# Average pooling over windows of four: an output tile with 64 KB stores on one queue, against three in-place input tiles with 16 KB stores on a second queue

## The chip, the core and the metric

The kernel runs on one core of a Trainium2 chip. The metric is the device time of one execution in microseconds. The core has 16 DMA engines that move data between the chip's memory (HBM) and the 128 partitions of its on-chip memory (SBUF); VectorE and ScalarE compute on what lies in SBUF. A DMA is issued by an instruction in the queue of some engine: SyncE (SP), which does nothing else here, or ScalarE. Instructions of one engine's queue are issued in order, and one that waits for a semaphore holds up all that stand behind it on the same engine.

## The reference

```python
x = np.random.randn(64, 256, 8192).astype(np.float32)   # kernel_size 4, stride 4
out_len = (length - kernel_size) // stride + 1
for i in range(out_len):
    start = i * stride
    output[:, :, i] = np.mean(x[:, :, start : start + kernel_size], axis=2)
```

Each output is the mean of four neighbouring floats, and the windows do not overlap. Since 8192 is a multiple of 4, rows need no special treatment: the input is one long list of floats, and output number j is the mean of inputs 4j to 4j + 3. 536.87 MB are read and 134.22 MB are written.

## The kernel before, in words

The 16384 rows of x are dealt to 128 partitions so that each partition holds 1,048,576 floats in all. The work is cut into 16 groups, and each group into 4 blocks (`LOADS`) of W = 16384 floats, 64 KB, per partition. In a group a partition owns 8 consecutive rows of x, 256 KB, and the views `xg` and `og` (lines 43 to 47) put them behind one another. So a load of one block (line 59) reads 64 KB from each of 128 places that lie 256 KB apart.

There are two input tiles (`xin`, line 49) and a single output tile (`res`, line 50), 64 KB per partition each. `sums` (lines 62 to 83) works on one block: VectorE adds neighbours, writing the 8192 results over the first half of the input tile (line 65), then adds neighbours of these into the block's quarter of the output tile (line 72). ScalarE scales the quarter by 1/4 in place (line 83). In the last block of a group the second sum and the scaling are cut in four, so that less remains after the last sum. Then one store (line 86) writes the whole output tile, 64 KB per partition, 8 MB.

All DMAs, loads and stores, are issued by SP (lines 59 and 86). The order there is written out by the loop of lines 97 to 112: the sums of block k, after a group's last block the store of the group, and then the load of block k + 2, which must wait until the sums of block k are done, as it takes their tile. The next group's second sum waits until the store has left the output tile. The DMA engines take what SP issued in the order of issue.

The end is cut finer. The last block is loaded in five pieces (line 92). The output of the last group's first two blocks is stored between the first and second of these loads (line 109); the third block's output is stored after the loads have been issued (line 114), which gives the DMA engines work while the last pieces are summed. The last two pieces are scaled on VectorE (line 79) and stored by the last instruction (line 121).

The lines that matter below are 59 (loads), 65 and 72 (the sums), 83 (the scaling) and 86 (the stores). Line 152 is the end of the program and line 138 its beginning.

Of the kernel before, what the change touches and what calls it, by code (L numbers as in the profile page):

```python
# [1 line left out]

# [4 lines left out]


LOADS = 4

LAST_CUTS = 4


@with_exitstack
def kernel(
    ctx: ExitStack,
    tc: tile.TileContext,
    x: bass.AP,
    kernel_size: bass.AP,
    stride: bass.AP,  # L20
    out: bass.AP,
):
    nc = tc.nc
    K, S = int(kernel_size), int(stride)
    assert K == S == 4
    B, C, L = x.shape
    P = nc.NUM_PARTITIONS
    add = mybir.AluOpType.add
    dt = x.dtype

    per = B * C * L // P
    W = 16384
    G = W * LOADS
    V = W // K
    groups = per // G
    assert per == groups * G

    xf = x.flatten_outer_dims()
    of = out.flatten_outer_dims()
    rows = G // L  # L40
    R = P * rows

    def xg(g):
        return xf[g * R : (g + 1) * R].rearrange("(p f) m -> p (f m)", f=rows)

    def og(g):
        return of[g * R : (g + 1) * R].rearrange("(p f) m -> p (f m)", f=rows)

    pin = ctx.enter_context(tc.tile_pool(name="xin", bufs=2))
    pout = ctx.enter_context(tc.tile_pool(name="res", bufs=1))  # L50

    state = {}

    def load(g, l, a, b):

        if a == 0:
            state["xt"] = pin.tile([P, W], dt, name="xt")
        xt = state["xt"]
        nc.sync.dma_start(out=xt[:, a:b], in_=xg(g)[:, l * W + a : l * W + b])  # L59
        return xt  # L60

    def sums(xt, ot, l, a, b, cuts, scale_on_dve=False):

        h = (a, (a + b) // 2)
        nc.vector.tensor_tensor(  # L65
            out=xt[:, h[0] : h[1]], in0=xt[:, a:b:2], in1=xt[:, a + 1 : b : 2], op=add
        )
        n = (b - a) // K
        for c in range(cuts):
            lo, hi = c * n // cuts, (c + 1) * n // cuts  # L70
            o = ot[:, l * V + a // K + lo : l * V + a // K + hi]
            nc.vector.tensor_tensor(  # L72
                out=o,
                in0=xt[:, a + 2 * lo : a + 2 * hi : 2],
                in1=xt[:, a + 2 * lo + 1 : a + 2 * hi : 2],
                op=add,
            )
            if scale_on_dve:
                nc.vector.tensor_scalar(  # L79
                    out=o, in0=o, scalar1=1.0 / K, scalar2=None, op0=mybir.AluOpType.mult  # L80
                )
            else:
                nc.scalar.mul(o, o, 1.0 / K)  # L83

    def store(g, ot, a, b):
        nc.sync.dma_start(out=og(g)[:, a:b], in_=ot[:, a:b])  # L86

    todo = [(g, l) for g in range(groups) for l in range(LOADS)]  # L90
    last = todo[-1]
    pieces = [W // 2, W // 4, W // 8, W // 16, W // 16]
    tiles = {}
    ot = None
    tiles[0] = load(*todo[0], 0, W)
    tiles[1] = load(*todo[1], 0, W)
    for k, (g, l) in enumerate(todo[:-1]):
        if l == 0:
            held, ot = ot, pout.tile([P, G // K], dt, name="ot")
        sums(tiles.pop(k), ot, l, 0, W, LAST_CUTS if l == LOADS - 1 else 1)  # L100
        if l == LOADS - 1:
            store(g, ot, 0, G // K)
        if k + 2 < len(todo) - 1:
            tiles[k + 2] = load(*todo[k + 2], 0, W)
        elif k + 2 == len(todo) - 1:

            n = pieces[0]
            lt = load(*last, 0, n)
            store(g, ot, 0, (l + 1) * V)
            for w in pieces[1:]:  # L110
                load(*last, n, n + w)
                n += w
    g, l = last
    store(g, ot, (l - 1) * V, l * V)
    edges = [sum(pieces[:i]) for i in range(len(pieces) + 1)]
    for a, b in zip(edges[:3], edges[1:4]):
        sums(lt, ot, l, a, b, 1)
    store(g, ot, l * V, l * V + edges[3] // K)
    for a, b in zip(edges[3:-1], edges[4:]):
        sums(lt, ot, l, a, b, 1, scale_on_dve=True)  # L120
    store(g, ot, l * V + edges[3] // K, (l + 1) * V)


# [1 line left out]
_INS = ['x', 'kernel_size', 'stride']  # L125
_OUTS = [((64, 256, 2048), 'float32')]

_NUMBERS = {'kernel_size': 4, 'stride': 4}


# [26 lines left out]
```

## Time and profile before

| what | value |
|---|---|
| three runs | 1558.01, 1558.77, 1560.35 us (median 1558.77) |
| the profiled execution's own time | 1560.02 us |
| its span, first to last instruction | 1558.2 us |
| ScalarE, line 83, 128x4096 | 48 times, 3616 ns each |
| VectorE, line 65, 128x8192 | 63 times, 8693 ns each |
| VectorE, line 72, 128x4096 | 48 times, 4425 ns each |
| median time from issue to landing, full loads | 26.9 us |
| the same, the 15 large stores | 24.5 us |

The profile is of one execution. Times inside it count from the start of the span; the run's own time is 1.8 us longer than the span. The DMA lines of the page give, for 40 equal slices of the span, the busy share of the 16 DMA engines in tenths. A "packet" there is one contiguous piece that one DMA engine moves: with these layouts one partition's part of a transfer is one packet, so a load of 8 MB is 128 packets of 64 KB, eight on each engine. At the end of its part of a transfer an engine writes a packet of four bytes that counts up a semaphore; those are the 1392 packets under 512 bytes, 16 for each of 87 transfers. The trace has a record of start, duration, queue and size for each packet.

### The profile page before, as it was taken

To read this page: it belongs to the slowest core of one execution; us is meant where nothing else is said; L and a number is where in the kernel's file an instruction comes from. 1 tells how busy PE (TensorE), PEld (TensorE's weight loads), DVE (VectorE), ACT (ScalarE), POOL (GpSimd) and SP (SyncE) were. 2 spreads that over 40 slices of the span, in tenths; PEclk is the share of its full clock that TensorE was granted. 3 is DMA by queue.
4 is the path that set the end of the run, shared out by engine and by line. 5 is a ranking of instruction groups with operands and counts; after the bars stand their busy time and mean duration, and the time that the engine had idled before them with its cause. 6 is when DMAs were issued, how large, how long until landed. Compare 5 with 4: busy or idle time off the path is not lost.

```text
span 1558.2 us, 522 instructions
## 1 busy us (share of the span) xinstructions
DVE 844.0 (54%) x183; ACT 241.9 (16%) x112; POOL 0.2 (0%) x4
## 2 busy tenths in 40 slices
DVE  3654636546365463654636546365463654636546
ACT  1111201112011120111201112011120111201111
POOL 0000000000000000000000000000000000000000
DMA  9999999999999999999999999999999999999998
GB/s 424 437 404 431 442 434 436 434 431 434 429 432 432 439 436 434 432 434 431 431 431 436 436 439 431 434 432 434 431 431 431 431 431 431 431 432 436 426 440 369
DMA packets 12532, 671.13 MB, mean 431 GB/s; under 512 B 1392, under 2 KB 1392, under 8 KB 1776
## 3 DMA queue, kind: packets, MB, share of 16 engines
q1 hardware_dynamic: 12528, 671.09, 99.8%
q14 instruction: 4, 0.03, 0.0%
HBM read 536.87 MB, written 134.22 MB: 431 GB/s over the span
## 4 chain that ended last, share of the span: by engine, by line
DMA 71%; DVE 27%; ACT 1%; SPq 0%; issue 0%
DMA xt<-in_x_dram 71%; DVE xt L65 18%; DVE ot L72 9%; ACT ot L83 1%; SPq L86 0%; SPq L59 0%; DVE ot L79 0%
## 5 line engine op out<-in xcount | busy, mean ns | idle before, releaser
L65 DVE TENSOR_TENSOR xt<-xt 128x8192 f32<-128x8192 f32 (+2 forms) x68 | 556.9, 8190 | 542.5 <-DMA xt<-in_x_dram 542.5
L83 ACT ACTIVATE ot<-ot 128x1024 f32<-128x1024 f32 (+3 forms) x111 | 240.6, 2167 | 1306.1 <-DVE ot L72 1302.6
L72 DVE TENSOR_TENSOR ot<-xt 128x1024 f32<-128x1024 f32 (+4 forms) x113 | 286.9, 2572 | 164.1 <-DMA out_dram<-ot 162.4
L83 ACT ACT_TABLE_LOAD x1 | 1.3, 1283 | 0.7 <-PEq L138 0.7
L79 DVE TENSOR_SCALAR ot<-ot 128x256 f32<-128x256 f32 x2 | 0.6, 291 | 0.0
L138 POOL MEMSET const-bfloat16-1.0<- 128x1 bf16 x1 | 0.1, 101 | 0.0
L138 POOL MEMSET const-uint8-127<- 128x1 uint8 x1 | 0.1, 101 | 0.0
L138 POOL MEMSET const-float32-0.0<- 128x1 f32 x1 | 0.1, 98 | 0.2 <-issue 0.2
L138 POOL MEMSET const-float32-1.0<- 128x1 f32 x1 | 0.1, 98 | 0.0
## 6 DMA issues: line engine op xcount, KB each, us to landing
xt<-in_x_dram SPq DMA_DIRECT2D x1, 4096.0 KB, 17.0
out_dram<-ot SPq DMA_DIRECT2D x1, 4096.0 KB, 23.0
xt<-in_x_dram SPq DMA_DIRECT2D x1, 2048.0 KB, 27.4
out_dram<-ot SPq DMA_DIRECT2D x1, 2048.0 KB, 18.4
out_dram<-ot SPq DMA_DIRECT2D x1, 1792.0 KB, 8.0
xt<-in_x_dram SPq DMA_DIRECT2D x1, 1024.0 KB, 29.4
xt<-in_x_dram SPq DMA_DIRECT2D x2, 512.0 KB, 30.6
xt<-in_x_dram SPq DMA_DIRECT2D x63, 26.9
```

Source lines behind the costliest of these rows:

```text
L65: nc.vector.tensor_tensor(out=xt[:, h[0] : h[1]], in0=xt[:, a:b:2], in1=xt[:, a + 1 : b : 2], op=add)
L72: nc.vector.tensor_tensor(out=o, in0=xt[:, a + 2 * lo : a + 2 * hi : 2], in1=xt[:, a + 2 * lo + 1 : a + 2 * hi : 2], op=add,)
L79: nc.vector.tensor_scalar(out=o, in0=o, scalar1=1.0 / K, scalar2=None, op0=mybir.AluOpType.mult)
L83: nc.scalar.mul(o, o, 1.0 / K)
L138: nc = _bacc.Bacc("TRN2", target_bir_lowering=False, num_devices=1)
```

## The change

The output tile goes, and with it groups. There are three input tiles of 64 KB (`BUFS_IN`), and both sums and the scaling of a block work inside its own tile: the block's 4096 means end up in the tile's first quarter. From there each block is stored by itself, 16 KB per partition, 2 MB in all. The store is issued from ScalarE's queue, right behind the scaling. SP issues the loads, and only two of the last stores: those of the last full block and of the first piece of the last block, which stand behind all loads.

A load now takes the tile of the block three earlier, so it waits for that block's store to have left. The loads run up to two blocks ahead of the block that is summed; once the first piece of the last block is loaded, the other pieces are issued at once.

The input is seen as one flat list. A block is 128 x 16384 consecutive floats, 64 KB for each partition, and the partitions' parts follow one another without gaps; the same holds for the stores, with 16 KB. The last block is cut in pieces of 8192, 4096, 2048, 1280 and 768 floats (before: 8192, 4096, 2048, 1024, 1024), each a contiguous block of its own, all in one tile. Only the last piece is scaled on VectorE.

The core of the diff (the old functions, printed above, go):

```diff
-LOADS = 4
-LAST_CUTS = 4
...
-    pin = ctx.enter_context(tc.tile_pool(name="xin", bufs=2))
-    pout = ctx.enter_context(tc.tile_pool(name="res", bufs=1))
...
+FULL = 16384
+BUFS_IN = 3
+HEAD = ()
+TAIL = (8192, 4096, 2048, 1280, 768)
+    assert L % K == 0
+    dt = x.dtype
+    xf = x.rearrange("b c l -> (b c l)")
+    of = out.rearrange("b c l -> (b c l)")
+    rest = B * C * L // P - sum(HEAD) - sum(TAIL)
+    assert rest % FULL == 0
+    blocks = [(w, i == 0) for i, w in enumerate(HEAD)]
+    blocks += [(FULL, True)] * (rest // FULL)
+    blocks += [(w, i == 0) for i, w in enumerate(TAIL)]
+    n = len(blocks)
+    first = n - len(TAIL)
+    pin = ctx.enter_context(tc.tile_pool(name="xin", bufs=BUFS_IN))
+    xs, begins = {}, [0]
+    for w, _ in blocks:
+        begins.append(begins[-1] + w)
+    def load(i):
+        w, fresh = blocks[i]
+        if fresh:
+            load.tile, load.at = pin.tile([P, FULL], dt, name="xt"), 0
+        a = load.at
+        load.at += w
+        src = xf[P * begins[i] : P * begins[i + 1]].rearrange("(p m) -> p m", p=P)
+        xs[i] = load.tile[:, a : a + w]
+        nc.sync.dma_start(out=xs[i], in_=src)
+    def means(i):
+        w, _ = blocks[i]
+        xt = xs.pop(i)
+        o = xt[:, : w // K]
+        nc.vector.tensor_tensor(out=xt[:, : w // 2], in0=xt[:, ::2], in1=xt[:, 1::2], op=add)
+        nc.vector.tensor_tensor(
+            out=o, in0=xt[:, : w // 2 : 2], in1=xt[:, 1 : w // 2 : 2], op=add
+        )
+        if i == n - 1:
+            nc.vector.tensor_scalar(
+                out=o, in0=o, scalar1=1.0 / K, scalar2=None, op0=mybir.AluOpType.mult
+            )
+        else:
+            nc.scalar.mul(o, o, 1.0 / K)
+        return o
+    def store(engine, i, o):
+        dst = of[P * begins[i] // K : P * begins[i + 1] // K]
+        engine.dma_start(out=dst.rearrange("(p m) -> p m", p=P), in_=o)
+    loaded = 0
+    for i in range(n):
+        while loaded < n and (loaded < i + BUFS_IN or loaded > first):
+            load(loaded)
+            loaded += 1
+        o = means(i)
+        store(nc.sync if i in (first - 1, first) else nc.scalar, i, o)
```

More of the change, by code (lines that the diff above doesn't have):

```diff
@@ L26 @@
     B, C, L = x.shape
+    assert L % K == 0
     P = nc.NUM_PARTITIONS
+    dt = x.dtype
     add = mybir.AluOpType.add
[L29 to L47, printed above, removed]
@@ L49 @@
-    pin = ctx.enter_context(tc.tile_pool(name="xin", bufs=2))
-    pout = ctx.enter_context(tc.tile_pool(name="res", bufs=1))
[L52 to L64, printed above, removed]
+    xf = x.rearrange("b c l -> (b c l)")
@@ L65, in sums @@
+    def means(i):
[3 more added lines that the diff above has]
+        nc.vector.tensor_tensor(out=xt[:, : w // 2], in0=xt[:, ::2], in1=xt[:, 1::2], op=add)
         nc.vector.tensor_tensor(
-            out=xt[:, h[0] : h[1]], in0=xt[:, a:b:2], in1=xt[:, a + 1 : b : 2], op=add
+            out=o, in0=xt[:, : w // 2 : 2], in1=xt[:, 1 : w // 2 : 2], op=add
         )
[L68 to L76, printed above, removed]
-            )
[L78 to L121, printed above, removed]
+        if i == n - 1:
+            nc.vector.tensor_scalar(
+                out=o, in0=o, scalar1=1.0 / K, scalar2=None, op0=mybir.AluOpType.mult
+            )
+        else:
+            nc.scalar.mul(o, o, 1.0 / K)
```

## The prediction

> **What bounds the kernel now.** I read the page's busy times first, then its DMA part, and then asked for the busy time of single stretches to see whether anything but the DMA engines ever sets the pace.
>
> ```profile
> span 1558.2 us, 522 instructions
> ...
> DVE 844.0 (54%) x183; ACT 241.9 (16%) x112; POOL 0.2 (0%) x4
> ...
> DMA  9999999999999999999999999999999999999998
> ...
> DMA packets 12532, 671.13 MB, mean 431 GB/s; under 512 B 1392, under 2 KB 1392, under 8 KB 1776
> ...
> q1 hardware_dynamic: 12528, 671.09, 99.8%
> ...
> HBM read 536.87 MB, written 134.22 MB: 431 GB/s over the span
> ```
>
> No compute engine is busy for more than 54% of the span, while the packets of the one DMA queue fill 99.8% of the time of all 16 DMA engines. The bytes are fixed by the problem, so the time is bytes over rate. The table of stretches shows that this holds inside every group of four blocks (columns: stretch, its length, busy time of VectorE, ScalarE and GpSimd, clock, DMA share, GB/s):
>
> ```profile
> 3.50:100.50 97.00, 52.68 (x11) 15.08 (x7) 0.00 (x0) 1.00 1.00 426
> 100.50:197.50 97.00, 52.68 (x11) 15.08 (x7) 0.00 (x0) 1.00 1.00 434
> 197.50:294.50 97.00, 52.68 (x11) 15.08 (x7) 0.00 (x0) 1.00 1.00 434
> ...
> 1361.50:1458.50 97.00, 52.67 (x11) 15.07 (x7) 0.00 (x0) 1.00 1.01 435
> ```
>
> A group takes 97 us, the DMA share is 1.00 and the rate 434 GB/s; only the first group (426) and the end are slower. The chain of waits says "DMA 71%; DVE 27%", which misleads if read alone: its DVE links are the path by which a buffer comes free, and while they run the DMA engines work on the other buffer's load. The wait list shows the same:
>
> ```profile
> DVE xt L65 <- DMA xt<-in_x_dram: 542.5, 64, 22.6
> DVE ot L72 <- DMA out_dram<-ot: 162.4, 15, 11.2
> ```
>
> The second line is the stall that three in-place buffers abolish: the sum into the single output tile waits about 11 us (162.4/15) in each group for the store of the group before. In those same groups the DMA share is 1.00, so it is worth nothing.
>
> So the question is what one byte costs in a DMA engine. Grouping the trace's packet records by size gives median durations: 64 KB 2418 ns, 32 KB 1213, 16 KB 611, 8 KB 309, 4 KB 159, 2 KB 84, and 9 ns for the four-byte packet with which each engine ends its part of a transfer. Halving a packet does not halve its time: 2 x 1213 - 2418 = 8 ns, (4 x 611 - 2418)/3 = 8.7 ns, 2 x 309 - 611 = 7 ns, 2 x 159 - 309 = 9 ns. **Each packet costs about 8 ns beside its bytes**, for loads and stores alike.
>
> **The change part by part.** All against the profiled execution: span 1558.2, run 1560.02.
>
> *Loads.* Before: 63 full loads of 128 packets of 64 KB and five pieces. After: the same 63 and five pieces of other widths (1280 and 768 columns for 1024 and 1024). Packets and bytes are equal: 0. The row pitch in memory falls from 256 KB to 64 KB ("contiguous blocks"). The 256 KB pitch already runs at 434 GB/s in a whole group, so there is little to win: I take 0.
>
> *Stores, packets.* Before: 19 stores of 128 packets, 15 of them with 64 KB packets, 2432 packets in all. After: 68 stores, 8704 packets, 63 x 128 of them 16 KB. That is 6272 more, 392 on each of the 16 engines, at 8 ns: **+3.1 us**. Nothing hides it, because the engines have no idle time. From above: 392 x 8.7 = 3.4. From below: if two queues let an engine overlap the end of one packet with the start of another's, the cost may vanish, and with it what before pays: (11136 data packets/16) x 8 ns = 5.6 us. So -5.6 to +3.4; I take +3.1, since it is the direct row.
>
> *Completion packets.* 136 transfers instead of 87: 49 more, one 9 ns packet on each engine: **+0.4 us**.
>
> *Turns between loading and storing.* Before turns 15 times in the steady part, after 63 times. A group of before is 40 packets per engine (4 loads and a store of 8 each): 40 x 2418 + 5 x 9 = 96.77 us. The issues of line 86 are 97.0 us apart ((1454.34 - 193.40)/13 from the timeline). The 0.23 us left holds one turn to the store and one back, and all jitter. If that is the price, 48 more turns cost 48 x 0.23 = +11 us; if the mixing of two queues has no such edge, 0. Where the price arises, the trace is specific: the rate summed from the packet records dips for some 2 to 4 us after a store joins loads (to 281 GB/s at the first store, near 97 us; 409 at the second), and stays at 433 or more where the next load follows the store. With two queues the packets lie side by side all the time and nothing changes over at once; also, 12 of the 15 dips lose under 0.25 us. I take **0** as the nearest row (store back to load), and keep +11 for the range.
>
> *The rule against the row.* The page DMA: Bandwidth & Descriptors of the Trainium skill, section "Latency and other measured facts" (HBM row pitch), gives 214 GB/s per direction as the full rate of copies of [128 x 16 KiB] tiles on the sync and scalar queues, thus 428 in both. Before's trace mixes queues nowhere and can't confirm it; the only figure here is 431 over the span. By the page, 671.09 MB/428 GB/s would be 1568 us of transfer, an estimate that speaks against this change. The same page, section "Issuing engines are not separate DMA queues", says that another issuing engine saves only issue time; no run here shows that either.
>
> *The in-place sums.* The big sums keep their forms (128x8192 at 8693 ns, 128x4096 at 4425 ns, ScalarE 3616 ns); the second sum's output moves into its own input buffer, as the first's always was. Per block VectorE works 8.69 + 4.42 = 13.1 us of some 24.3: 0 while the DMA engines are full. The two scalings of the tail on VectorE become one.
>
> *The added wait.* A load now waits, on SP, for the store of the block three earlier; behind it on SP are only further loads. Is it late? A block is ready for its store 13.1 + 3.6 + 0.4 = 17.1 us after landing (line 65, 72, 83 and an issue). A period is now 8 x 2418 + 8 x 611 + 18 = 24.25 us of each DMA engine. If the store's eight packets alternate with eight load packets, the store takes up to 24.2 us more: it ends 41.3 us after the landing. The two loads queued in that time last until 48.5 us. So the next load is issued some 7 us early, less a few us for issue and landing. And were it late, the next block's store, ready at 24.25 + 17.1 = 41.4 us on the same count, would be in the other queue to fill the gap. I see no hole: 0, and if the cover fails for half the blocks by 1 us each, +30 would be the sum; no row suggests it. ScalarE has only its next scaling behind each store's issue (24% busy at most).
>
> *Start and end.* First data comes 1.9 us into the span in both, and the first 64 KB packets take some 3000 ns. At the end, before loses 2.4 us of engine time in the last 8 us, and 0.8 us near 1522. After keeps 2 MB and 1 MB of stores on SP behind the last loads, 3 MB/0.434 = 7.2 us of cover for the last pieces, whose sums take about 4 us after the last landing. Either kernel ends with full engines and a straggler: 0, give or take 1.5.
>
> Sum: 3.1 + 0.4 = +3.5 us, span 1561.7. The profiled run was 1560.02 and lies 1.25 us above the median 1558.77, with spread 2.3 among the three; I add to the median: **1562.3 us**.
>
> **Rivals.**
> *A, the packets count and nothing else* (chance 0.52): +2 to +4.5, about 1562.3. For it: equal durations for loads and stores, full engines. Some packets overlap slightly in the records, so +3.5 is rather a high value, and part of A (0.27 of the 0.52) lies inside 0.2% of the median, which is about what a measurement of this kernel can tell from no change: 1555.7 to 1561.9.
> *B, turns cost* (0.27): each block's store disturbs the loads as a store does now, at 0.23 us: 1562.3 + 11 = 1573. It sets the result once a turn costs over 0.1 us (48 x 0.1 = 4.8, more than the packets). For it: the dips at the first stores. Against it: they shrink, and are absent on the way back. If every one of the 8 packets of a block turned at that price, 63 x 8 x 0.23 = +116; I give that 0.03 of the 0.27.
> *C, two queues hide the gaps between packets* (0.18), **on the other side, faster**: the place is the 8 ns between two packets of one queue on one engine. If a packet of the second queue fills it, the whole 5.6 us that before pays goes, and none is added: 1558.8 - 5.6 + 0.4 = 1553.6. All gaps of after would be 5.6 + 3.1 = 8.7 us; it ends faster from the point where 3.5/8.7, two in five of them, are filled. For it: a few records of before overlap at a turn without loss. Against it: where they overlap, each takes longer.
> *D, the change does not do what it says* (0.03): the waits put stores and loads in step, so that a queue stays empty for a while; within B's times.
>
> **How the numbers follow.** A is likeliest: 1562.3. To hold 8 in 10 the range takes in C's 1553.6 and B's 1573: 1552 to 1574; A alone would be 1560.5 to 1563.5. Faster by over 0.2%: most of C, 0.15. Within: 0.27 of A and the rest of C, 0.30. Slower: the rest of A, B and D, 0.55.
>
> **What would show it.** Packets: 17408 data, 2176 completions and the 4 of the other queue, 19588 on the page. A second queue with 16 KB packets near 611 ns; if they and the 64 KB ones last longer while the engines hold two at a time, judge by GB/s. Before takes 97.0/4 = 24.25 us per block in the steady part; A makes it 24.25 + 3.5/63 = 24.31, B 24.31 + 11/63 = 24.48, C 24.25 - 5.2/63 = 24.17. VectorE's wait for stores should be gone and its wait for loads grown by about as much. The prediction is wrong if the DMA share falls visibly below 0.99 (a hole, the added wait), if the steady rate leaves 430 to 434, or if the end differs by over 2 us.

## The result, and the profile after

The changed kernel takes 1556.16 us (median of 20 runs, 1555.92 to 1556.69), the kernel before 1559.51 in the 20 runs beside them (1558.01 to 1560.35). The ratio is 0.998, 95% interval 0.9974 to 0.9986: **faster by 3.3 us**, where 3.5 us slower was forecast; 0.2%, small but clear of the noise. The changed kernel also varies less from run to run, by 0.8 us against 2.3.

The page of the changed kernel, the lines that answer to those of before:

```profile
span 1554.3 us, 580 instructions
...
DVE 840.5 (54%) x137; ACT 233.1 (15%) x68; POOL 0.2 (0%) x4
...
DMA packets 19590, 671.14 MB, mean 432 GB/s; under 512 B 2177, under 2 KB 2433, under 8 KB 2945
...
q1 hardware_dynamic: 10080, 540.02, 80.3%
q10 hardware_dynamic: 9504, 131.08, 19.7%
```

VectorE is still busy for 54% of the span and the DMA engines are full, now with a second queue (q10) for a fifth of their time. The packets are as many as predicted (19588, and two more of the small third queue). The same four stretches as before:

```profile
3.50:100.50 97.00, 47.21 (x7) 12.13 (x4) 0.00 (x0) 1.00 0.99 424
100.50:197.50 97.00, 53.32 (x10) 14.46 (x4) 0.00 (x0) 1.00 1.00 434
197.50:294.50 97.00, 52.75 (x9) 14.46 (x4) 0.00 (x0) 1.00 1.00 433
...
1361.50:1458.50 97.00, 52.82 (x9) 14.46 (x4) 0.00 (x0) 1.00 1.01 435
```

The rate of a stretch has not risen visibly, though the bytes are now carried by more packets. The wait list, VectorE's only wait for DMA and SP's largest:

```profile
DVE xt L67 <- DMA xt<-in_x_dram: 705.0, 64, 22.6
```

```profile
SPq L61 <- DMA out_dram<-xt: 1490.8, 61, 64.6
```

VectorE's 162.4 us of waiting for stores are gone, and its wait for loads grew by the same 162.5 us (542.5 to 705.0): the stall was worth nothing, as the prediction said. SP now waits for stores nearly all the time, which costs nothing as long as the DMA engines have loads in hand (DMA share 1.00 above).

Where did 3.9 us of the span go? The steady part shows little to the eye, so I added up the packet records. In the table, *nominal* is each data packet at the usual time of its size (64 KB 2418 ns, 16 KB 611, and so on), *excess* what packets took beyond it, *overlap* the time in which more than 16 packets were in flight, *holes* that with fewer; all as us per DMA engine. From the first packet to the last, wall = nominal + completions + excess - overlap + holes.

| kernel | data packets per engine | nominal | completions | excess | overlap | holes | wall |
|---|---|---|---|---|---|---|---|
| before | 696 | 1548.0 | 0.8 | 6.4 | 2.8 | 2.9 | 1555.3 |
| after | 1088 | 1551.4 | 1.2 | 1.6 | 4.6 | 1.7 | 1551.3 |

The predicted cost is there: nominal +3.4 and completions +0.4. Three terms outweigh it: excess -4.8, overlap -1.8, holes -1.2. The excess by stretches of 97 us says more: before it is 0.47 us in the first 3.5 us, 1.54 in the first stretch, 0.11 to 0.65 in each of the following 14, and 1.28 from there to the end; after it is 0.64, 0.82, 0.00 to 0.04 in each of the 14, and 0.08. From 100 us on, packets of the changed kernel are late by 0.2 us in all. Both rows are of one execution each: that of before lies 0.5 us above its median, and another execution of the changed kernel (the last of the experiments) has an excess of 2.6, with nearly all of the difference in its first 100 us.

### The profile page after: what moved, and what is told of

The parts are those of the page before. It is cut to its first block, busy times and chain, and to the rows that moved or that the text cites. A ratio compares the mean times of both kernels' runs of the same rounds, so it can differ in the third digit from the quotient of the medians.

```text
span 1554.3 us, 580 instructions
## 1 busy us (share of the span) xinstructions
DVE 840.5 (54%) x137; ACT 233.1 (15%) x68; POOL 0.2 (0%) x4
## 4 chain that ended last, share of the span: by engine, by line
DMA 76%; DVE 19%; ACT 5%; issue 0%; DVEq 0%; SPq 0%
DMA xt<-in_x_dram 39%; DMA out_dram<-xt 37%; DVE xt L67 12%; DVE xt L68 6%; ACT xt L76 5%; DVEq L67 0%; SPq L61 0%; DVE xt L72 0%
## 5 line engine op out<-in xcount | busy, mean ns | idle before, releaser
L67 DVE TENSOR_TENSOR xt<-xt 128x8192 f32<-128x8192 f32 (+2 forms) x68 | 556.8, 8190 | 705.0 <-DMA xt<-in_x_dram 705.0
L76 ACT ACTIVATE xt<-xt 128x4096 f32<-128x4096 f32 (+2 forms) x67 | 231.8, 3461 | 1291.5 <-DVE xt L68 1291.5
L68 DVE TENSOR_TENSOR xt<-xt 128x4096 f32<-128x4096 f32 (+2 forms) x68 | 283.7, 4174 | 2.2
```

Of the source, the lines that this page charges most:

```text
L67: nc.vector.tensor_tensor(out=xt[:, : w // 2], in0=xt[:, ::2], in1=xt[:, 1::2], op=add)
L68: nc.vector.tensor_tensor(out=o, in0=xt[:, : w // 2 : 2], in1=xt[:, 1 : w // 2 : 2], op=add)
```

## The experiments

Four theories of the gain stood at first: Q, the second queue (packets of two queues overlap, changes from loading to storing vanish); S, small and evenly spread stores, whichever the queue; L, the contiguous blocks; E, the end. Times are medians; the kernel before, run beside them, had 1558.75 us in the first set of four, 1559.12 in the second, 1558.27 in the third and 1558.25 in the last. So a difference between two sets is good to some 0.9 us.

**One queue.**

```diff
-        store(nc.sync if i in (first - 1, first) else nc.scalar, i, o)
+        store(nc.sync, i, o)
```

> The changed kernel with every store issued by SP instead of ScalarE, so that all DMAs are in one queue; store of block i stands behind the load of block i + 2. Everything else is as in the changed kernel (1556.2 us). Theory Q (the gain comes from the second queue: packets of two queues overlap, and bulk turns from loading to storing vanish): the gain goes and the extra packets stay, 1559.5 + 3.5 = about 1562 to 1563. Theory S (the gain comes from small, evenly spread stores, whichever queue they are in): 1556 to 1557. Theory L (the gain comes from the contiguous blocks): 1556 to 1557. Theory E (the gain comes from the end): 1556 to 1557, since the end's order on SP is kept.

1594.42 us (ratio 1.0221, 1.0196 to 1.0246). S is out, and the price is six times what Q allowed. Bytes and packets are those of the changed kernel; the excess is 39.1 us instead of 1.6, the overlap 4.4 against 4.6. The stretches of this kernel, columns as before:

```profile
100.00:400.00 300.00, 162.27 (x26) 44.49 (x13) 0.00 (x0) 1.00 1.01 432
400.00:700.00 300.00, 157.41 (x24) 43.63 (x13) 0.00 (x0) 1.00 1.00 420
700.00:1000.00 300.00, 157.41 (x24) 44.65 (x13) 0.00 (x0) 1.00 1.00 419
```

The DMA share stays 1.00 while the rate falls to 420 GB/s: the engines are never idle, their packets take longer. Which packets, the records around one change from loading to storing show (packets in flight, mean duration of those that started):

```
us          loads  stores   64 KB load   16 KB store
647 to 648   16.0     0.0      2418 ns
649 to 650   16.1     0.0      3296
651 to 652   15.7     0.0      3823
653 to 654    6.2     9.9                    611 ns
656 to 657    0.0    16.1                    611
```

The last load packets of all engines are late, most of them by 0.9 to 1.6 us, just before the first stores start (652.7 us) and as they do; the stores themselves are on time. There are 30 such change-overs, for a load waits for a store here and so loads and stores go in pairs of blocks. The first costs 1.1 us, the next five 0.03 to 0.3, and each of the other 24 from 0.9 to 1.5: 30.8 us in all. The way back to loads costs another 5.4 us, at most 0.4 each.

**The old pitch.** Loads and stores at the places of the kernel before, four blocks of a partition together:

```diff
+    def strided(flat, by, i):
+        g, at = divmod(begins[i], 4 * FULL)
+        part = flat[P * g * 4 * FULL // by : P * (g + 1) * 4 * FULL // by]
+        part = part.rearrange("(p m) -> p m", p=P)
+        return part[:, at // by : (at + blocks[i][0]) // by]
...
-        src = xf[P * begins[i] : P * begins[i + 1]].rearrange("(p m) -> p m", p=P)
+        src = strided(xf, 1, i)
...
-        dst = of[P * begins[i] // K : P * begins[i + 1] // K]
-        engine.dma_start(out=dst.rearrange("(p m) -> p m", p=P), in_=o)
+        engine.dma_start(out=strided(of, K, i), in_=o)
```

> The changed kernel with the row pitch of the kernel before: four blocks of a partition lie together, 256 KB apart for loads and 64 KB for stores; queues, tiles and sizes as in the changed kernel. Theory L: 2 to 3 us of the gain go, 1558.5 to 1559.5. Theories Q, S and E: 1556.2 within 0.5.

1558.42 us (1557.17 to 1560.91; ratio 1.0001, 0.9992 to 1.001), 2.3 us more than the changed kernel: L holds, and against the kernel before nothing is left of the gain. The spread of the runs is back as well. In the profiled execution, one of the fastest, the excess is 3.1 us against 1.6, and each stretch of 97 us after the first has 0.01 to 0.26 of it. That execution took 1557.17 us; where the slower ones lose more, no profile shows.

**All stores on ScalarE.**

```diff
-        store(nc.sync if i in (first - 1, first) else nc.scalar, i, o)
+        store(nc.scalar, i, o)
```

> The changed kernel with all stores on ScalarE's queue, those of the last full block and of the first piece of the last block too, which SP issued behind the loads. Theory E (the end is where the gain is, by these two stores as cover): 1 to 3 us slower, 1557 to 1559. Theories Q, S and L: the stores are as many and the DMA engines find them in the other queue, 1556.2 within 0.5.

1556.16 us: the same as the changed kernel. E is out as far as the two late stores go; the rest of the end was not varied.

**Stores in halves.**

```diff
-        engine.dma_start(out=dst.rearrange("(p m) -> p m", p=P), in_=o)
+        dst = dst.rearrange("(p m) -> p m", p=P)
+        h = blocks[i][0] // K // (2 if i < first else 1)
+        for a in range(0, blocks[i][0] // K, h):
+            engine.dma_start(out=dst[:, a : a + h], in_=o[:, a : a + h])
```

> The changed kernel with each store of a full block cut in two of 8 KB per partition, both on ScalarE's queue: 63 x 128 packets more, 504 on each engine, and up to 63 completion packets. If a packet of the second queue costs the 8 ns that the kernel before shows: 504 x 8 ns = 4.0 us plus 63 x 9 ns = 0.6, so 1560.8. If theory Q holds and gaps are filled by the other queue's packets: under 1558.

1574.29 us, 18.1 more than the changed kernel: neither answer. Of this the nominal time is 3.5 us and the completions 0.6, but the excess grew by 15.2. The packets that start in each 2.5 us tell why:

```
              changed kernel          stores in halves
us            loads   stores          loads   stores
602.5            16       16              3       58
605.0            16       16              0      127
607.5            16       16              0      128
615.0            19        2             17        0
620.0            10        9             18        0
635.0            16       14             15       14
```

While both queues of the changed kernel have work, 16 load and 16 store packets start in the same time, as if each of the 16 engines took one packet of each queue in turn (the records do not name the engine). A block has 8 load and 8 store packets per engine, so its store lasts about as long as a load from issue to landing (the last column, us):

```profile
out_dram<-xt ACTq DMA_DIRECT2D x62, 2048.0 KB, 27.7
...
xt<-in_x_dram SPq DMA_DIRECT2D x63, 28.1
```

The next store is there as one ends: between 100 and 1500 us, loads are in flight without a store for 6.6 us at most and stores without a load for 1.6. With 16 store packets against 8 load packets the store cannot keep up at one to one. The loads run out of tiles, the stores then run alone (29 times, 4.4 us each), and the engines change over again. Of the 14.6 us of excess between 100 and 1500 us, 10.5 lie at these change-overs. That is a new theory, R: the two queues' packet numbers balance. It has a rival, P: 8 KB packets in the second queue are dear by themselves.

**Loads and stores in halves.** The same edit, and for the loads

```diff
-        nc.sync.dma_start(out=xs[i], in_=src)
+        h = w // (2 if i < first else 1)
+        for a in range(0, w, h):
+            nc.sync.dma_start(out=xs[i][:, a : a + h], in_=src[:, a : a + h])
```

> The changed kernel with loads cut in two (32 KB packets) and stores cut in two (8 KB packets): 16 packets of each queue per block and engine, so that the numbers are equal again. Theory R (each engine takes packets of the two queues in turn, one by one; with equal numbers a block's store lasts as long as a load, and there is never a change-over from loading to storing; with twice as many store packets the loads ran out of tiles and the engines changed over, which cost 18 us): the 18 us vanish, and what is left is at most 1008 packets x 8 ns = 8.1 us and 126 completions = 1.1 us: 1558 to 1565.5, no stretch in which only stores run. Rival P (8 KB packets in the second queue are dear by themselves, 18 us/504 = 36 ns each): 1574 or more.

1561.37 us: R holds and P falls, since the same stores cost 13 us less once the loads have as many packets. The stretches of the kernel with half stores, and then of this one:

```profile
100.00:400.00 300.00, 162.34 (x26) 43.39 (x12) 0.00 (x0) 1.00 1.00 426
400.00:700.00 300.00, 159.37 (x25) 47.01 (x13) 0.00 (x0) 1.00 1.00 427
700.00:1000.00 300.00, 160.03 (x25) 43.39 (x12) 0.00 (x0) 1.00 1.00 428
```

```profile
100.00:400.00 300.00, 162.89 (x26) 46.74 (x13) 0.00 (x0) 1.00 1.01 433
400.00:700.00 300.00, 158.08 (x25) 43.66 (x13) 0.00 (x0) 1.00 1.00 432
700.00:1000.00 300.00, 166.01 (x26) 43.39 (x12) 0.00 (x0) 1.00 1.00 432
```

More packets and a higher rate. The run also gives the price of a packet: 1561.37 - 1556.16 = 5.2 us for 1008 packets and 126 completions (1.1 us), 4.1 ns each, within some 0.9 us for the whole, as the two runs are of different sets. The records show the rest of the 8 ns as overlap.

**Loads in halves alone.** The second edit without the first.

> The changed kernel with loads cut in two (32 KB packets), stores as they are: 16 load packets for 8 store packets per block and engine. Theory R: a store now lasts 8 x (1213 + 611) ns = 14.6 us and is followed by loads alone; the loads never run out of tiles, but an engine goes from mixed work to loads alone and back in each block. 504 packets x 8 ns = 4.0 us and 0.6 for completions: 1558 to 1561, a few us more if the way from loads alone back to mixed work costs anything. Rival P: the same, as no packet of a store changes.

1560.21 us, inside the range: +4.0 for 504 packets and 63 completions. Stores run for half of a block's time, then loads alone for some 10 us, and the return to mixed work costs about 0.01 us each time. So it is not every change that costs, and the packet numbers of the two queues need not be equal. By the time, a packet costs (4.0 - 0.6)/504 = 6.9 ns here; 1.0 us of excess and 0.4 of holes are in it.

**Contiguous blocks in the kernel before.** Its tiles, its one queue, its stores of four blocks:

```diff
...
-        nc.sync.dma_start(out=xt[:, a:b], in_=xg(g)[:, l * W + a : l * W + b])
+        nc.sync.dma_start(out=xt[:, a:b], in_=xb(g * LOADS + l)[:, a:b])
...
+            dst = of[k * P * V : (k + n) * P * V].rearrange("(l p m) -> p l m", l=n, p=P)
+            nc.sync.dma_start(out=dst, in_=ot[:, a:b].rearrange("p (l m) -> p l m", l=n))
...
```

> The kernel before with the contiguous blocks of the changed kernel, and nothing else of it: one queue, two input tiles, one output tile, one store for a group of four blocks. Since a block's output is now contiguous, that store consists of 512 pieces of 16 KB instead of 128 of 64 KB; the number of transfers stays. Theory L (the pitch is worth what putting the old pitch into the changed kernel cost, 2.3 us, in any kernel), with the full price of packets, 15 x 3 x 8 = 360 on each engine x 8 ns = 2.9 us: 1558.75 - 2.3 + 2.9 = about 1559.4. If small packets cost nothing even in one queue: 1556.5. If contiguous blocks pay only together with two queues: 1561.6.

1563.35 us, 4.2 more than before (ratio 1.0029, 1.0018 to 1.0041), above all three answers and nearest to the third. Nominal +3.2, excess +1.3, and 1.5 us more of overlap to set against them: where engines still change over, the contiguous blocks show no gain. Their spread is small, though, 1562.97 to 1564.18.

**A mixture.** Two input tiles and two output tiles of 32 KB, each stored for two blocks with 32 KB packets by ScalarE's queue:

```diff
-LOADS = 4
+LOADS = 2
...
-LAST_CUTS = 4
+LAST_CUTS = 1
...
-    pout = ctx.enter_context(tc.tile_pool(name="res", bufs=1))
+    pout = ctx.enter_context(tc.tile_pool(name="res", bufs=2))
...
-            store(g, ot, 0, G // K)
+            store(g, ot, 0, G // K, nc.scalar)
...
```

> A mixture: two input tiles of 64 KB as in the kernel before, two output tiles of 32 KB for two blocks each, stored with 32 KB packets by ScalarE's queue; pitch 128 KB; the end's pieces and stores are those of the kernel before without its early store. 252 packets on each engine fewer than in the changed kernel. Theory R: 8 store packets stand against 16 load packets, so a store lasts 8 x (2418 + 1213) ns = 29 us of the 48.5 us of two blocks; change-overs every two blocks. Between 1556.2 - 2.0 (packets) and, with the pitch half as dear as 256 KB and some change-overs, 1559.

1568.99 us (1559.89 to 1580.34): missed. The nominal time is 2.4 us lower, the excess 15.3. Loads run alone for 21 us between two stores; the return to mixed work costs, but for the first (1.1 us), 0.00 to 0.1 us until 650 us into the span and 0.1 to 1.1 us in the rest. Stretches of this kernel:

```profile
100.00:400.00 300.00, 162.07 (x26) 47.01 (x13) 0.00 (x0) 1.00 1.01 436
400.00:700.00 300.00, 165.95 (x25) 43.40 (x12) 0.00 (x0) 1.00 1.00 431
```

Fewer packets do bring 436 GB/s while nothing is late, and then it is lost.

**Two input tiles and four output tiles** of 16 KB, in the same memory:

```diff
-BUFS_IN = 3
+BUFS_IN = 2
...
+    pout = ctx.enter_context(tc.tile_pool(name="res", bufs=4))
...
-        w, _ = blocks[i]
+        w, fresh = blocks[i]
...
-        o = xt[:, : w // K]
+        if fresh:
+            means.tile, means.at = pout.tile([P, FULL // K], dt, name="ot"), 0
+        o = means.tile[:, means.at : means.at + w // K]
+        means.at += w // K
```

> The changed kernel with two input tiles of 64 KB and four output tiles of 16 KB in place of three in-place tiles, in the same 192 KB per partition; blocks, stores, queues and end as in the changed kernel. A load then waits for the sums of the block two earlier and not for a store. If the in-place tiles are only one way to have both queues filled: 1556.2 within 0.5. If it matters that a load waits for a store (it keeps the two queues in step): the change-overs come back, 1560 or more.

1555.85 us (1555.54 to 1556.3), ratio 0.9984 (0.9976 to 0.9993): as good as the changed kernel, with the same budget (excess 1.7, overlap 4.6). The three in-place tiles are not what brings the gain.

**Small stores in one queue, with the old tiles.**

```diff
-        if l == LOADS - 1:
-            store(g, ot, 0, G // K)
         if k + 2 < len(todo) - 1:
             tiles[k + 2] = load(*todo[k + 2], 0, W)
+            if g < groups - 1:
+                store(g, ot, l * V, (l + 1) * V)
```

> The kernel before (its tiles, its pitch, one queue) with a store of 16 KB packets for each block, issued by SP behind the load of block k + 2. In one queue all engines change over from loads to a store and back in each block. Theory R (a change-over costs; the kernel before pays about 0.2 us for each of its 15, the one-queue form of the changed kernel 1.2 us for most of its 30): 1558.5 as in the changed kernel with the old pitch, plus 60 x 0.2 to 60 x 1.2: 1570 to 1630. Rival T (it was the shortage of tiles that cost time in the one-queue form, as its loads waited for stores; here they do not): 1558 to 1561.

1772.81 us, outside both. The excess is 42.6 us, about 0.7 for each of 60 change-overs and within R's bounds, but the engines also had nothing to do for 178 us, some 12 in each group. Its page and its timeline (start, length, engine, line, [idle before]) show both:

```profile
q1 hardware_dynamic: 19008, 671.10, 90.0%
```

```profile
446.76 8.69 DVE L65 TENSOR_TENSOR xt<-xt 128x8192 f32<-128x8192 f32 x1 [11.62 <-DMA xt<-in_x_dram]
472.42 8.69 DVE L65 TENSOR_TENSOR xt<-xt 128x8192 f32<-128x8192 f32 x1 [16.97 <-DMA xt<-in_x_dram]
481.02 8.75 DVE L72 TENSOR_TENSOR ot<-xt 128x4096 f32<-128x4096 f32 x2
```

After the first sum of a group's first block (446.76) the second does not follow: it needs the single output tile, whose last store now stands behind a load on SP. The next block's first sum goes ahead, the second sums of both come at 481, and until then no tile is free for a load. The order of line 102 before line 104 in the kernel before avoids just that. As a measure of a change-over this run is spoiled, and with it the test of rival T: whether one queue costs as much where no load waits for a store is not settled.

**A pitch of 4 MB.** As the second experiment, with 64 blocks together.

> The changed kernel with the rows of a partition all in one piece, so that a load reads 64 KB from each of 128 places 4 MB apart, and a store writes at places 1 MB apart; everything else as in the changed kernel (64 KB pitch: 1556.2; 256 KB pitch: 1558.4). If what 256 KB costs grows with the pitch: some us to hundreds of us more than 1558.4. If it comes from the step into a new group every four blocks, of which there are none here: 1556.2 to 1557. The Trainium skill, page DMA: Bandwidth & Descriptors, section Latency and other measured facts (HBM row pitch), gives 103 GB/s in each direction for a pitch of 4 MiB, which would make 3258 us of 671 MB.

2386.43 us. The price grows with the pitch. The page:

```profile
DMA packets 19589, 671.14 MB, mean 280 GB/s; under 512 B 2176, under 2 KB 2432, under 8 KB 2944
...
q1 hardware_dynamic: 10080, 540.02, 86.7%
q10 hardware_dynamic: 9504, 131.08, 12.9%
```

The 64 KB load packets take 4073 ns in the median instead of 2418, the 16 KB stores, 1 MB apart, still 611. The Trainium skill (DMA: Bandwidth & Descriptors, section "Latency and other measured facts", HBM row pitch) gives 103 GB/s in each direction at 4 MiB, for 16 KiB pieces. That would be 206 in both together, an estimate; the 280 measured here are for 64 KB reads, with a quarter as many bytes written as read. The page's list begins at 512 KiB with nearly the full rate (207 of 214). At 256 KB, which it does not list, the price here was 2.3 us.

**Loads or stores?** The old pitch on one side only, and the changed kernel once more beside them.

> The changed kernel with the old pitch for the loads alone (64 KB pieces 256 KB apart), and contiguous stores. The means of a block are thus stored at other places than the reference has them; the amount of work is the same. If the 2.3 us that the old pitch cost come from the loads: 1558.4. If from the stores' places or from both falling together: 1556.2 to 1557.

> The changed kernel with the old pitch for the stores alone (16 KB pieces 64 KB apart), and contiguous loads; here too the means land at other places than the reference has them. If the cost of the old pitch comes from the stores: 1558.4. If from the loads: 1556.2.

> The changed kernel once more, as the measure for the two beside it on the same chip: 1556.2 within 0.3 by every theory, and 0.998 of the kernel before.

Loads 1558.55 us (1556.98 to 1559.89), stores 1556.36 (1555.98 to 1556.98), changed kernel 1556.14 (1555.95 to 1557.42). The loads' pitch carries the price and the spread of the runs.

## Why the prediction was wrong

The bound was read rightly, and the counts of packets and completions came true. The sum had the wrong sign because of three of its terms, those of the loads, the stores' packets and the turns.

- **Loads, "Packets and bytes are equal: 0 ... there is little to win".** This failed: the pitch is worth 2.3 us (1558.42 or 1558.55 against 1556.16). That is most of the net gain of 3.3 us, and all of the 2.1 us in the last set (1558.25 against 1556.14). A whole group at 434 GB/s was taken as proof of no loss, but 2.3 us are 0.15%, 0.6 GB/s, less than that view resolves. The packet records show 1.1 us of it in a fast execution: between 100 and 1459 us, late packets make 1.1 us with the old pitch and 0.1 without.
- **Stores' packets, "+3.1 us".** Mis-sized: 4.1 ns a packet where both sides were halved, not 8, so 392 x 4.1 = 1.6 us, as much as nominal less overlap in the table (3.4 - 1.8). Durations of single packets were added although neighbours overlap by some 4 ns each; 2.8 us/696 in the kernel before could have been read from its records.
- **Turns, "48 more turns", price 0 to +11.** The count failed. In the kernel after, packets of one kind are never alone in flight for more than 6.6 us, and so the price of the turns of before goes too. In the profiled execution of before, 3.9 of the 6.4 us of excess lie at its 15 large stores: 1.4 where the first store joins the loads, 1.1 at the other 14, and 1.5 where the loads follow again, up to 0.5 each late in the span. The prediction took the way back as its row because it had read no loss there; that holds for the early turns only. Zero was not a floor; the term should have reached below it by what before pays. How much of the gain in the medians this is stays rough: the old pitch with two queues and the kernel before differ by only 0.3 us (1558.42 against 1558.75), and in that the former bears the 3.4 + 0.4 - 1.8 = 2.0 us of its additional packets.
- **End, "0, give or take 1.5".** Slightly missed, by the records. From 1500 us to the last packet, before has 0.9 us of late packets, most of them at the store issued at 1514.77, and 2.4 us of holes; after has 0.1 and 1.4. That is 1.9 us of the 3.9, about as much as the pitch is worth in the medians. The two late stores on SP are not the reason (1.5 us of holes without them, 1.7 with them, in the whole span), and no run gave the kernel before the end of the kernel after.
- **Completions +0.4, in-place sums 0, the added wait 0**: right. Two input tiles, whose loads wait for no store, give 1555.85.

In numbers: 3.4 + 0.4 - 1.8 - 4.8 - 1.2 = -4.0 us by the records, -3.9 in span; the medians of 20 differ by 3.3. These terms are of one execution each, and the executions of the kernel before differ by 2.3 us.

Rival C named the right side and, by luck, nearly the right block time: 24.17 us, measured (1519.57 - 116.22)/58 = 24.20 between starts of line 67. But its mechanism fell: the overlap per packet is 2.8/696 = 4.0 ns before, 4.6/1088 = 4.2 after, and 4.4/1088 = 4.0 in the one-queue form. A second queue hides no gap that one queue does not. Rival B's mechanism is real, at up to 1.5 us a turn, in the kernel with one queue, where some 36 of the 38 us lie at its turns; with two queues that keep up with each other there is next to nothing for it to act on. So the second issuing queue saved more here than the time of issuing. And the estimate of 1568 us from 428 GB/s is answered: after the first 100 us, the stretches shown of both kernels run at 433 to 435 GB/s, and the changed kernel's 1556.16 us is 12 us below it.

What stays open: why a change from loading to storing is nearly free at one time and costs a microsecond at another. But for the very first, it is cheap in the first 300 us of the one-queue form, in the first 650 of the mixture and throughout where loads are halved (loads alone for 10 us), and dear later on. The lateness begins before the first store packet starts, and no run shows what causes it. The kernel before with nothing but its stores moved to the second queue was not run. Nor is it settled why a 256 KB pitch delays loads, nor why contiguous blocks gave nothing in one queue.

## What to carry to other kernels

Where the DMA engines are full, compare, over several executions, the sums of packet times beyond the usual time of their size, not rates by stretch: tenths of a per cent are invisible in the latter. Put loads and stores in two queues, and let the stores have no more packets per round than the loads, so that the loads never run out of tiles behind them: splitting the stores alone cost 18 us here, splitting both 5 and splitting the loads alone 4. That alone is not enough: the mixture, with half as many store packets as load packets, lost 13 us. And lay blocks out so that what one load reads is contiguous, even where a large pitch seems to run at full rate.

## What the runs showed of the hardware

With work in two queues, the engines started as many packets of one as of the other, whatever their sizes: 16 of 64 KB and 16 of 16 KB in 2.5 us. Late packets are nearly all loads: where the one-queue form changed over, the last 64 KB loads took up to 4.1 us in place of 2.42, while the 16 KB stores beside them kept their 611 ns. Changes from load to store packet within a few us are not dear: the changed kernel makes them all the time, and its packets were late by 0.2 us in all after the first 100 us. And small packets are cheaper than their durations suggest, 4 ns each instead of 8 where both sides were halved.
